# 272-token tiles padded to a multiple of 256 bytes, and the big buffers moved by 128 bytes against the weights

## The chip, the cores and the metric

The kernel runs on one core of one Trainium2 chip. The metric is the device time of one execution in microseconds; of several runs the median is given. A profile is one more execution, recorded by the hardware profiler; its span is the time from its first instruction to its last.

## The reference

One transformer block on 256 tokens of width 2048, with 16 meta tokens put in front (272 in all), in float32: a feed-forward block, a mixer with a pooling branch and a latent attention branch, and a second feed-forward block. Cut to what matters:

```python
h = concat([meta, x])                                   # 272 x 2048
h = h + 0.5 * rmsnorm(swiglu(rmsnorm(h), w_gu, w_down)) # 2 x 5632 columns, then 5632 rows
z = rmsnorm(h) @ w_in                                   # pool, c_q, c_kv, k_rope, two gates
y_pool = multiscale_pool(u_pool) @ w_pool_o
y_mla = attention(c_q @ w_q_b, c_kv @ w_kv_b, rope) @ w_mla_o
h = h + rmsnorm((sigmoid(g_pool) * y_pool + sigmoid(g_mla) * y_mla) @ w_out)
h = h + 0.5 * rmsnorm(swiglu(rmsnorm(h), w_gu2, w_down2))
return h[16:]
```

From the second half of the mixer on only the last 256 tokens are carried.

## The kernel before

Activations lie transposed: features on the 128 partitions, tokens along the free dimension, one tile per 128 features. A float32 product is made from parts of 12 bits: weight and input are each split into a high and a low part (`hi` and `lo`), and three products are added: high by high, high by low, low by high. With 272 tokens (`L`) these are three matmuls of 272 columns (`mm3`, lines 213 to 215). With 256 tokens (`R`) they are two (`mm_wide`): line 219 takes both parts of the input side by side, 512 columns, and line 221 the high part with the low part of the weight, 256 columns.

The weights are one stream of 128 x 128 tiles in the order of their use (class `Weights`). The DMA queue of SP loads chunks of `CH` = 8 tiles (512 KB) into one of `RAW` = 5 buffers (line 79). A part is `PT` = 4 tiles; for each part ACT makes the high half (line 92) and DVE the low half (line 93) in one of `HL` = 6 buffers. All this is issued by `take`, which is called once per tile just ahead of its matmuls:

```python
self.load((p + HL - 1) * PT // CH + RAW)
self.divide(p + min(HL - 1, p // 2 + 2))
```

So the splits of the weights stand in the queues of ACT and DVE between the work that empties PSUM. Each engine keeps the order in which its instructions are issued. `Later` delays work by a number of steps of the weights' stream.

Inputs of products are kept by class `Two`: eight tiles in a big buffer, each with its high part and then its low part. The big buffers come from one pool (`slot`, `SLOT` = 16 x 272 floats each, nine of them); one of them holds the residual stream `h` for the whole run. `big`, `raw`, `parts` and `tmp` (temporaries of 272 floats) lie one after another in the on-chip memory, the small ones ahead of them.

`products` runs over output tiles: where a block begins, `wave` = 6 of them side by side (their PSUM tiles are named `w`), with the input tiles coming up to date one by one (`Stream`), and then one by one (`m`), each over all input tiles. Names in the profile: `x` is a block's input, `a` the input of w_down, `o` the heads' output, `y` the gated sum, `po` the pooling branch's output product, `CB` the latent vectors of the attention. At the end of a block `post` and `advance` make the norm and the next input; `load_table` loads ACT's table of functions.

Of the kernel before, what the change touches and what calls it, by code (L numbers as in the profile page):

```python
# [27 lines left out]
CH, PT = 8, 4  # L28
RAW, HL = 5, 6
WARM = (3, 7)  # L30
# [6 lines left out]
C_COS, C_SIN, C_MASK, C_KPE, C_FREE = 0, 272, 544, 960, 1232  # L37
SLOT = KD * L


class Nothing:
    """Stands in for the builder's objects while the order of the weights is collected."""

# [16 lines left out]
class Weights:  # L60
    """The weights as one stream of [128, 128] tiles in the order of their use; each chunk of CH
    tiles is loaded ahead, and split, PT tiles at a time, into two parts of 12 bits, which together
    are the float32."""

# [32 lines left out]
    def take(self, *tiles):  # L97
        """The next tiles of the stream, side by side."""
        n = len(tiles)
        room = PT - len(self.order) % PT  # L100
        if room < n:
            self.order += [None] * room
        at = len(self.order)
        self.order += tiles
        if self.plan is None:
            return Nothing(), Nothing()
        assert self.plan[at : at + n] == list(tiles)
        p, j = divmod(at, PT)
        self.load((p + HL - 1) * PT // CH + RAW)
        self.divide(p + min(HL - 1, p // 2 + 2))  # L110
        for _ in tiles:
            self.tick()
        hi, lo = self.split[p]
        s = slice(j * P, (j + n) * P)
        return hi[:, s], lo[:, s]


class Later:
    """Work that is issued some steps of the weights' stream later, so that an engine isn't held
    by what another one has yet to do."""  # L120

# [3 lines left out]
    def __call__(self, *steps):  # L125
        """steps: pairs of a delay after the one before, and what to run then."""
        at = self.now
        for delay, run in steps:
            at += delay
            self.due.append((at, run))  # L130
        self.due.sort(key=lambda d: d[0])
# [11 lines left out]
def build(nc, tc, ctx, hT, wsrc, gains_d, const_d, tables_d, out, order):  # L143
# [7 lines left out]
    parts = ctx.enter_context(tc.tile_pool(name="parts", bufs=HL))  # L151
    big = ctx.enter_context(tc.tile_pool(name="big", bufs=9))
    tmp = ctx.enter_context(tc.tile_pool(name="tmp", bufs=6))
    psum = ctx.enter_context(tc.tile_pool(name="psum", bufs=8, space=bass.MemoryType.PSUM))
# [4 lines left out]
    def slot(cols, dt, name):  # L159
        t = big.tile([P, SLOT], dt, tag="S", name=name)  # L160
        return t[:, :cols]
# [9 lines left out]

# [1 line left out]
    h = slot3(KD, L, F32, "h")  # L173
    gains = keep.tile([P, NG], F32, tag="gains", name="gains")
# [19 lines left out]
    class Two:  # L194
        """n tiles of T tokens in two parts of 12 bits, side by side."""

        def __init__(self, n, T, name, src=None):
            self.T, self.at = T, 16 * T
            self.s = [src or slot(self.at, F32R, f"{name}{i}") for i in range(-(-n // 8))]
            self.s = [a[:, : self.at].rearrange("p (a b c) -> p a b c", a=8, b=2) for a in self.s]  # L200

# [15 lines left out]
    def mm_wide(b, w, x, k, first, last):  # L217
        """The same with the product of the low part of x in columns of its own, from R on."""
        mm(b.rearrange("p (b c) -> p b c", b=2), w[0], x.both(k, R), start=first, stop=last,  # L219
           skip_group_check=True)  # L220
        mm(b[:, :R], w[1], x.hi(k, R), start=False, stop=last, skip_group_check=True)  # L221

    def join(b, s):
        """s: the sum of both halves of b, in two steps."""
        act(s, b[:, R:], AF.Copy)
        return GAP, lambda: dve.tensor_tensor(s, b[:, :R], s, op=ALU.add)

    def warm(n, x=ident):
        """Keeps the tensor engine's clock up while it has to wait."""
        b = bank("warm")  # L230
        for _ in range(n):
            mm(b[:, :P], x[:, :P], x[:, :P], start=True, stop=True)

# [1 line left out]
    def rms_sums(sources, T, n, half=False):  # L235
        """1 / sqrt(mean + eps), or half of it, of the tokens whose squares' sums over the
        partitions of `sources` add up to n * mean; the tokens are on partitions."""
        b = bank("rms")
        tt = (0, P, L - P)[: 3 if T == L else 2]
        m, c0 = len(tt), 400  # L240
        for i, s in enumerate(sources):
            for j, t0 in enumerate(tt):
                mm(b[:, c0 + j : c0 + j + 1], s[:, t0 : t0 + P], ones[:, :1],
                   start=i == 0 and j == 0, stop=i == len(sources) - 1, skip_group_check=True)
        sd = tmp.tile([P, 4], F32, tag="sd", name="sd", bufs=2)
        f = 4 if half else 1
        act(sd[:, :m], b[:, c0 : c0 + m], AF.Sqrt, scale=f / n, bias=eps[:, f // 4 : f // 4 + 1])
        dve.reciprocal(sd[:, :m], sd[:, :m])
        return b, sd

    def rms_spread(b, sd, T):
        """The same for all partitions, in the bank's first T columns."""
        for j, (t0, c) in enumerate(((0, 0), (P, 0), (L - P, P - NMETA))[: 3 if T == L else 2]):
            mm(b[:, t0 + c : t0 + P], sd[:, j : j + 1].to_broadcast([P, P]), ident[:, c:],
               start=True, stop=True)
# [8 lines left out]
    def squares(src, T, j, last=False):  # L264
        """Adds the squares of src to acc; the last ones stay apart, for `rms` to add."""
        if j == 0:
# [11 lines left out]

# [1 line left out]
    class Stream:  # L280
        """The residual stream's parts for the next products; `update` brings a tile of it up to
        date. Issued in stages that lead the products by a tile."""

# [18 lines left out]
        def scale(self):  # L302
            """The pre-norm's scales; products of the unscaled input are scaled by them."""
            b, sd = rms_sums([acc] + self.last, self.T, DM)
# [6 lines left out]
    def products(names, n_k, x, T, wave, evac, stream=None, hooks={}, narrow=()):  # L311
        """Tiles of x @ w, transposed: the first `wave` of them side by side, then one by one."""
        wide = [T == R and i not in narrow for i in range(len(names))]
# [32 lines left out]

# [1 line left out]
    def post(names, n_k, x, T, g_post, half, wave, wait):  # L348
# [26 lines left out]

# [1 line left out]
    def ffn(x, w_gu, w_down, g_post, wait):  # L377
# [27 lines left out]

    # ================= first feed-forward =================
    warm(10, zero)
# [8 lines left out]

    # ================= mixer =================
    x = advance(t, b, L, G_MPRE)
# [15 lines left out]
    def rotate(o, src, T):  # L434
        """Rotary embedding of rows [x1, x2, x1, x2] of 32 each; o may not be src."""
        c = slice(L - T, L)
# [33 lines left out]
    def windows(j):  # L470
        """Difference of the windows' means and the input, in parts."""
        w = WINDOWS[j // 2]
# [19 lines left out]

    # columns of w_in in tiles: c_kv, k_rope twice, c_q, u_pool
    names = [("w_in", ("kv", j)) for j in range(4)] + [("w_in", ("kr", 0))]
# [57 lines left out]

# [1 line left out]
    o2 = Two(HEADS, R, "o")  # L554
# [40 lines left out]
    def proj_v(g):  # L595
        """Rows of v of four heads: tokens 0.., tokens 128.., and those from 256 on, by the high
        part of the input in rows 64.. and by the low part in rows 80.. ."""
        bs = [bank(f"v{i}") for i in range(3)]
# [47 lines left out]
    def turn(i):  # L646
        """Transposes the probabilities: keys 128.. and keys 0.. of the two times 128 queries. Of
        the first 128 queries' keys from 128 on only 16 exist, the rows below are zero; the second
        ones' keys from 256 on go to rows 64.. and again to rows 80.. of the last columns."""
        b = bank("pt")  # L650
# [49 lines left out]

# [1 line left out]
    y = Two(KD, R, "y")  # L702
# [17 lines left out]

    # ================= second feed-forward =================
    t, b = ffn(advance(t, b, R, G_F2PRE), "ffn2_w_gu", "ffn2_w_down", G_F2POST, (0, 0))
# [15 lines left out]
def columns(name, m):  # L738
    """Columns of a weight that make its tile m."""
    a = np.arange(P)  # L740
# [71 lines left out]
```

## Time and profile before

| | |
|---|---|
| time, median of 3 runs | 2244.32 us (2243.51 to 2244.43) |
| span of the profiled execution | 2257.5 us, granted PE clock 0.998 |
| PE busy | 2234.3 us (99%), 15040 matmuls |
| weight loads busy | 2062.4 us (91%) |
| DVE / ACT / POOL busy | 1362.2 / 1142.5 / 205.4 us |
| DMA | 393.46 MB, mean 174 GB/s, 53.7% of 16 engines' time for the weights' queue |

The profiled execution is 13.2 us (0.6%) longer than the median run. PE's rows are matmuls, PEld's the loads of their weights, which overlap them. A matmul's duration reaches from its start to its modelled end and overlaps the next one's, so the pace is read from one start to the next. In a tile's rows the columns are: line, engine, operation, out<-in, count, duration in ns (least, median, greatest), first and last start in us, shapes.

### The profile page before, as it was taken

To read this page: it belongs to the slowest core of one execution; us is meant where nothing else is said; L and a number is where in the kernel's file an instruction comes from. 1 tells how busy PE (TensorE), PEld (TensorE's weight loads), DVE (VectorE), ACT (ScalarE), POOL (GpSimd) and SP (SyncE) were. 2 spreads that over 40 slices of the span, in tenths; PEclk is the share of its full clock that TensorE was granted. 3 is DMA by queue.
4 is the path that set the end of the run, shared out by engine and by line. 5 is a ranking of instruction groups with operands and counts; after the bars stand their busy time and mean duration, and the time that the engine had idled before them with its cause. 6 is when DMAs were issued, how large, how long until landed. Compare 5 with 4: busy or idle time off the path is not lost.

```text
span 2257.5 us, 39449 instructions
## 1 busy us (share of the span) xinstructions
PE 2234.3 (99%) x15040; PEld 2062.4 (91%) x15040; DVE 1362.2 (60%) x2456; ACT 1142.5 (51%) x2273; POOL 205.4 (9%) x229
## 2 busy tenths in 40 slices
PE   9999999999999999999999999999999999999997
PEld 9999999999999999988888888888888888888886
DVE  6555555555444477766666677577666666654554
ACT  6444444444444454555544555665555555554543
POOL 2000000000000053200121111150000000000001
PEclk9999999999999999999999999999999999999999
DMA  6555555555555545566533356545655555655553
GB/s 242 178 175 174 179 172 178 177 170 177 177 169 180 175 150 168 178 190 188 173 113 122 114 169 195 186 151 186 185 188 184 188 186 186 187 191 187 187 182 117
DMA packets 109311, 393.46 MB, mean 174 GB/s; under 512 B 12288, under 2 KB 13696, under 8 KB 109120
## 3 DMA queue, kind: packets, MB, share of 16 engines
q1 hardware_dynamic: 108576, 389.19, 53.7%
q8 instruction: 118, 1.93, 0.4%
q0 software_dynamic: 400, 1.61, 0.2%
q14 instruction: 73, 0.60, 0.1%
q10 hardware_dynamic: 144, 0.13, 0.0%
HBM read 388.78 MB, written 2.10 MB: 173 GB/s over the span
## 4 chain that ended last, share of the span: by engine, by line
PE 97%; DVE 2%; issue 1%; DMA 0%; ACT 0%; SPq 0%; ACTq 0%; DVEq 0%
PE m L219 29%; PE m L221 15%; PE m L213 13%; PE m L215 12%; PE m L214 12%; PE w L219 2%; PE w L214 1%; PE w L221 1%; PE w L215 1%; PE s L622 1%; PE w L213 1%; PE po L213 1%; PE po L215 1%; PE po L214 1%; PE s L621 1%
## 5 line engine op out<-in xcount | busy, mean ns | idle before, releaser
L93 DVE TENSOR_TENSOR lo<-raw,hi 128x512 fp32r<-128x512 f32 x1472 | 1042.9, 722 | 691.7 <-ACT hi L92 686.7
L92 ACT ACTIVATE hi<-raw 128x512 fp32r<-128x512 f32 x1472 | 882.5, 625 | 393.6 <-PE m L214 283.1
L219 PE MATMUL m<-x,hi 128*128 128x512 f32 x1824 | 643.3, 398 | 0.0
L221 PE MATMUL m<-x,lo 128*128 128x256 f32 x1824 | 513.0, 281 | 0.0
L213 PE MATMUL m<-x,hi 128*128 128x272 f32 (+1 forms) x1488 | 429.6, 289 | 0.0
L215 PE MATMUL m<-x,lo 128*128 128x272 f32 (+1 forms) x1488 | 429.2, 288 | 0.0
L214 PE MATMUL m<-x,hi 128*128 128x272 f32 (+1 forms) x1488 | 428.4, 288 | 0.0
L219 PEld LDWEIGHTS m<-x,hi 128*128 128x128 f32 x1824 | 342.9, 188 | 83.2
L221 PEld LDWEIGHTS m<-x,lo 128*128 128x128 f32 x1824 | 345.0, 189 | 0.0
L214 PEld LDWEIGHTS m<-x,hi 128*128 128x128 f32 x1488 | 282.9, 190 | 0.0
L213 PEld LDWEIGHTS m<-x,hi 128*128 128x128 f32 x1488 | 279.8, 188 | 0.0
L215 PEld LDWEIGHTS m<-x,lo 128*128 128x128 f32 x1488 | 279.7, 188 | 0.0
L219 PE MATMUL m<-a,hi 128*128 128x512 f32 x660 | 233.2, 399 | 0.0
L273 POOL TENSOR_TENSOR acc<-acc,sq 128x272 f32<-128x272 f32 (+1 forms) x88 | 83.4, 948 | 1532.8 <-ACT sq L270 1532.5
L215 PE MATMUL m<-a,lo 128*128 128x272 f32 (+1 forms) x748 | 215.7, 288 | 0.0
L213 PE MATMUL m<-a,hi 128*128 128x272 f32 (+1 forms) x748 | 215.7, 288 | 0.0
L214 PE MATMUL m<-a,hi 128*128 128x272 f32 (+1 forms) x748 | 215.3, 288 | 0.0
L221 PE MATMUL m<-a,lo 128*128 128x256 f32 x660 | 185.4, 281 | 0.0
L219 PEld LDWEIGHTS m<-a,hi 128*128 128x128 f32 x660 | 124.1, 188 | 31.1
L214 PEld LDWEIGHTS m<-a,hi 128*128 128x128 f32 x748 | 142.4, 190 | 0.0
L213 PEld LDWEIGHTS m<-a,hi 128*128 128x128 f32 x748 | 140.8, 188 | 0.0
L215 PEld LDWEIGHTS m<-a,lo 128*128 128x128 f32 x748 | 140.8, 188 | 0.0
(206 smaller groups left out, 2577.4 us busy)
## 6 DMA issues: line engine op xcount, KB each, us to landing
raw<-w SPq DMA_DIRECT2D x735, 512.0 KB, 3.5
h<-hT POOLq DMA_DIRECT2D x4, 272.0 KB, 5.7
out<-t SPq DMA_DIRECT2D x8, 128.0 KB, 1.9
out<-t SPq DMA_DIRECT2D x4, 256.0 KB, 2.1
h<-hT SPq DMA_DIRECT2D x1, 544.0 KB, 9.1
raw<-w SPq DMA_DIRECT2D x2, 256.0 KB, 3.5
MA<-tables POOLq DMA_DIRECT2D x1, 480.0 KB, 3.7
h<-hT SPq DMA_DIRECT2D x2, 136.0 KB, 2.9
```

Of the source, the lines that this page charges most:

```text
L92: nc.scalar.activation(hi, t, AF.Copy)
L93: nc.vector.tensor_tensor(lo, t, hi.bitcast(F32), op=ALU.subtract)
L213: mm(o, wh, xh, start=first, stop=False)
L214: mm(o, wh, xl, start=False, stop=False)
L215: mm(o, wl, xh, start=False, stop=last)
L219: mm(b.rearrange("p (b c) -> p b c", b=2), w[0], x.both(k, R), start=first, stop=last, skip_group_check=True)
L221: mm(b[:, :R], w[1], x.hi(k, R), start=False, stop=last, skip_group_check=True)
L273: pool_e.tensor_tensor(acc[:, :T], acc[:, :T], s[:, :T], op=ALU.add)
L621: mm(b[:, c : c + n], q[:, t0 : t0 + P], k[:, :n], start=True, stop=False)
L622: mm(b[:, c : c + n], qp[hp : hp + 64, t0 : t0 + P], kpe[hp : hp + 64, :n], start=False, stop=True)
```

## The change

- `Two` gives each tile of 272 tokens `SIDE` = 32 floats of room behind its two parts, so that the step from tile to tile is 2304 bytes instead of 2176. Tiles of 256 tokens keep a step of 2048 bytes.
- A big buffer is `ROOM` = 18432 bytes instead of 17408. `h` gets a buffer of its own in a new pool ahead of the big ones, with 32 floats more than it needs; the pool `big` keeps eight buffers. By these sizes every big buffer now begins 128 bytes after a multiple of 256 bytes counted from the weights' parts; before it was 0.
- To make room, `RAW` goes from 5 to 4, `HL` from 6 to 5, and the temporaries from 6 to 5. Other sizes and the order of the matmuls are the same.
- Comments are gone and lines are numbered anew: lines 79, 92, 93 are 81, 94, 95 after; 213 to 215 are 219 to 221, and 219 and 221 are 225 and 227.

```diff
-RAW, HL = 5, 6
+RAW, HL = 4, 5
...
 SLOT = KD * L
+SIDE = 32
+ROOM = 8 * (2 * L + SIDE)
...
-    big = ctx.enter_context(tc.tile_pool(name="big", bufs=9))
-    tmp = ctx.enter_context(tc.tile_pool(name="tmp", bufs=6))
+    own = ctx.enter_context(tc.tile_pool(name="own", bufs=1))
+    big = ctx.enter_context(tc.tile_pool(name="big", bufs=8))
+    tmp = ctx.enter_context(tc.tile_pool(name="tmp", bufs=5))
...
-        t = big.tile([P, SLOT], dt, tag="S", name=name)
+        t = big.tile([P, ROOM], dt, tag="S", name=name)
...
-    h = slot3(KD, L, F32, "h")
+    h = own.tile([P, SLOT + SIDE], F32, tag="h", name="h")[:, :SLOT].rearrange("p (a b) -> p a b", a=KD)
...
         def __init__(self, n, T, name, src=None):
-            self.T, self.at = T, 16 * T
+            self.T, self.step = T, 2 * T + (SIDE if T == L else 0)
+            self.at = 8 * self.step
             self.s = [src or slot(self.at, F32R, f"{name}{i}") for i in range(-(-n // 8))]
-            self.s = [a[:, : self.at].rearrange("p (a b c) -> p a b c", a=8, b=2) for a in self.s]
+            self.s = [a[:, : self.at].rearrange("p (a c) -> p a c", a=8)[:, :, : 2 * T]
+                      .rearrange("p a (b c) -> p a b c", b=2) for a in self.s]
```

With `HL` smaller, each split stands one part earlier in the list of its engine's other work. ACT's instructions at the switch from w_mla_o to w_out (1397 us in the profile; `hi883` is the high half of part 883, `raw441` its chunk), before:

```order
L92 ACTIVATE hi882_16273<-raw441_16139 128x512
L711 ACTIVATE y1_15326<-zm_11200 128x256
L92 ACTIVATE hi883_16288<-raw441_16139 128x512
L225 ACTIVATE sum_16301<-m_16243 128x256
L711 ACTIVATE y1_15326<-zm_11200 128x256
L277 ACT_TABLE_LOAD
L277 ACTIVATE small_102<-eps_97 128x1
L92 ACTIVATE hi884_16316<-raw442_16166 128x512
L92 ACTIVATE hi885_16330<-raw442_16166 128x512
```

and after:

```order
L94 ACTIVATE hi881_16270<-raw440_16148 128x512
L717 ACTIVATE y1_15321<-zm_11195 128x256
L94 ACTIVATE hi882_16283<-raw441_16179 128x512
L231 ACTIVATE sum_16296<-m_16238 128x256
L717 ACTIVATE y1_15321<-zm_11195 128x256
L283 ACT_TABLE_LOAD
L283 ACTIVATE small_103<-eps_98 128x1
L94 ACTIVATE hi883_16313<-raw441_16179 128x512
L94 ACTIVATE hi884_16325<-raw442_16208 128x512
```

Before, part 883 is split ahead of the last sums and of the table load, after, behind them. The same on ACT at the second feed-forward's switch to w_down (1995 us), before:

```order
L394 ACTIVATE gu_22557<-gu_22557 128x256
L92 ACTIVATE hi1298_22589<-raw649_22456 128x512
L92 ACTIVATE hi1299_22603<-raw649_22456 128x512
L225 ACTIVATE gu_22615<-m_22559 128x256
L398 ACTIVATE a5_17309<-gu_22615 128x256
L277 ACT_TABLE_LOAD
L277 ACTIVATE small_102<-eps_97 128x1
L92 ACTIVATE hi1300_22625<-raw650_22483 128x512
```

and after:

```order
L400 ACTIVATE gu_22552<-gu_22552 128x256
L94 ACTIVATE hi1297_22586<-raw648_22466 128x512
L94 ACTIVATE hi1298_22598<-raw649_22495 128x512
L231 ACTIVATE gu_22610<-m_22554 128x256
L404 ACTIVATE a5_17304<-gu_22610 128x256
L283 ACT_TABLE_LOAD
L283 ACTIVATE small_103<-eps_98 128x1
L94 ACTIVATE hi1299_22622<-raw649_22495 128x512
```

Here part 1299 moves behind the table load. DVE's list moves in the same way. PE's list of matmuls, and SP's list of DMAs, are the same as before but for the buffers' numbers.

## The prediction

> **What bounds the kernel now.** I read the head of the page first, then the chain that ended last, then who made TensorE (PE) wait.
>
> ```profile
> span 2257.5 us, 39449 instructions
> ...
> PE 2234.3 (99%) x15040; PEld 2062.4 (91%) x15040; DVE 1362.2 (60%) x2456; ACT 1142.5 (51%) x2273; POOL 205.4 (9%) x229
> ...
> PEclk9999999999999999999999999999999999999999
> ...
> PE 97%; DVE 2%; issue 1%; DMA 0%; ACT 0%; SPq 0%; ACTq 0%; DVEq 0%
> ...
> L219 PE MATMUL m<-x,hi 128*128 128x512 f32 x1824 | 643.3, 398 | 0.0
> L221 PE MATMUL m<-x,lo 128*128 128x256 f32 x1824 | 513.0, 281 | 0.0
> ```
>
> PE is busy 99% of the span at a full granted clock, 97% of the chain is PE, and its big groups have no idle time before them. So what counts is the distance from one matmul's start to the next one's (durations overlap). Who PE waited for:
>
> ```profile
> PE w L219 <- DVE x L298: 3.6, 7, 0.7
> PE w L214 <- DVE x L298: 2.8, 6, 0.5
> PE warm L232 <- DVE zero L178: 1.2, 1, 1.2
> ```
>
> Under 8 us in all, at the start and where a block's output is added to the residual stream. The time is the pace of back-to-back matmuls. It stands in the rows of a tile, each with its count and the first and last start; in order: tile x at 60 to 580 us, tile a, tile x at 1050 to 1100 us, tile o, tile y, tile x at 1530 to 1990 us:
>
> ```profile
> L213 PE MATMUL m<-x,hi x1276: 284/288/293, 60.0 to 540.3; 128*128 128x272 f32 x183
> ...
> L219 PE MATMUL m<-a,hi x660: 394/398/404, 1992.7 to 2225.6; 128*128 128x512 f32 x165
> ...
> L219 PE MATMUL m<-x,hi x144: 392/394/397, 1049.7 to 1099.7; 128*128 128x512 f32 x144
> ...
> L219 PE MATMUL m<-o,hi x224: 390/391/392, 1316.6 to 1394.0; 128*128 128x512 f32 x112
> ...
> L219 PE MATMUL m<-y,hi x144: 394/398/404, 1428.1 to 1478.6; 128*128 128x512 f32 x144
> ...
> L219 PE MATMUL m<-x,hi x1303: 394/398/404, 1529.9 to 1989.9; 128*128 128x512 f32 x187
> ```
>
> Last start minus first, over the count less one: a **triple** of 272-token matmuls (lines 213, 214, 215) takes 480.3/1275 = 376.7 ns. A **pair** (512 columns at 219, 256 at 221) takes 460.0/1302 = 353.3 ns in the second feed-forward's x, 232.9/659 = 353.4 in a, 50.5/143 = 353.1 in y, but 77.4/223 = 347.1 in o and 50.0/143 = 350 in the gates. All are the same instructions; the pace differs by 2%.
>
> **Where the operands lie.** By the sizes in the code, every weight tile starts at the same place modulo 256 bytes (steps of 512, buffers of 4096 and 2048), and the big buffers (17408 = 68 x 256) too. So before, a 256-token operand lies 0 bytes from its weights modulo 256. A 272-token one steps by 2176 = 8.5 x 256: even tiles have their high part at 0 and their low part at 64, odd ones at 128 and 192. After, 272-token tiles are all at 128 and 192, 256-token ones at 128 (both parts); the gates, which read the last 256 of 272 tokens, go from 64 or 192 to 192 throughout.
>
> Does it matter? Two triples in a row of the first feed-forward, from the timeline (start, duration in us):
>
> ```profile
> 399.78 0.29 PE L213 MATMUL m<-x,hi 128*128 128x272 f32 x1
> ...
> 400.16 0.28 PE L213 MATMUL m<-x,hi 128*128 128x272 f32 x1
> ```
>
> Line 213's durations alternate between the ends of its 284 to 293 ns: along the order of the tiles the short ones (and triples of 372 ns) are the odd tiles, the long ones (381 ns) the even. But the mean need not move if all become odd: in the six side-by-side tiles at the start of the block, one input tile is used six times running. Starts of the first matmul of x tile 12, of tile 13 (odd), of the third triple of 13, and of tile 14:
>
> ```profile
> 35.41 0.29 PE L213 MATMUL w<-x,hi 128*128 128x272 f32 x1
> ...
> 37.67 0.29 PE L213 MATMUL w<-x,hi 128*128 128x272 f32 x1
> ...
> 38.42 0.29 PE L213 MATMUL w<-x,hi 128*128 128x272 f32 x1
> ...
> 39.94 0.29 PE L213 MATMUL w<-x,hi 128*128 128x272 f32 x1
> ```
>
> Even after even: 2.26/6 = 376.7 ns a triple. Odd after odd: 2.27/6 = 378.3, and its last four 1.52/4 = 380. So the gain of the odd tiles seems to be the other side of the even ones' loss.
>
> **The change part by part.**
> 1. *Pitch of 272-token tiles.* The triples that come one after another, from the groups by shape:
>
> ```profile
> L213 PE MATMUL m<-x,hi 128*128 128x272 f32 x1440 | 416.0, 289 | 0.0
> ...
> L213 PE MATMUL m<-a,hi 128*128 128x272 f32 x704 | 203.2, 289 | 0.0
> ```
>
> 2144 in all. Bounds from rows: all like the odd ones between even ones, 372 (-4.7 ns, -10.1 us), and all like the end of tile 13, 380 (+3.3, +7.1 us). I take 378.3, the odd-after-odd mean, since that is the layout after: 2144 x 1.6 = **+3.4 us**.
> 2. *256-token operands from 0 to 128.* Long pace: 1824 less the gates' 512 on x, 660 on a, 144 on y, and 2 x 96 side by side on x and y = 2308. No row shows a pair at 128. Bounds: the best pace of any pair, 347.1 (-6.2 ns, -14.3 us), and as far above 353.3 as that lies below, +14.3 us. I take 350, the nearest pairs that are not at 0 (the gates): 2308 x -3.3 = **-7.6 us**; and o's 256 pairs (with 32 side by side) from 347.1 to 350 too, **+0.7 us**. Gates, attention and narrow products change offset within what they span now: 0, within a microsecond or two.
> 3. *HL from 6 to 5.* Every split of a weight part (ACT's line 92, VectorE's (DVE) 93) is issued one part later. A part is four pairs, 1.41 us. Mostly this only shortens a lead: paired part by part along the stream, low parts are ready a median of 5.0 us ahead of their first use. Three places have under 1.41 us, each behind an activation table load. The clearest (ACT, PE, DVE rows, in order of time):
>
> ```profile
> 1397.08 1.28 ACT L277 ACT_TABLE_LOAD   x1
> ...
> 1398.46 0.39 PE L219 MATMUL w<-y,hi 128*128 128x512 f32 x1
> ...
> 1398.48 2.18 ACT L92 ACTIVATE hi<-raw 128x512 fp32r<-128x512 f32 x4
> ...
> 1398.69 0.28 PE L221 MATMUL w<-y,lo 128*128 128x256 f32 x1
> ...
> 1399.13 1.90 DVE L93 TENSOR_TENSOR lo<-raw,hi 128x512 fp32r<-128x512 f32 x3 [1.61 <-ACT hi L92]
> ...
> 1399.85 0.40 PE L219 MATMUL w<-y,hi 128*128 128x512 f32 x1
> ```
>
> Now the first split behind the load makes part 884, used from 1399.85 on. After, it makes 883, used from 1398.46, whose low part (ready at 1399.83) PE wants at 1398.69: 1.1 us of waiting. The same at the second feed-forward's switch to w_down:
>
> ```profile
> 1996.56 3.96 ACT L92 ACTIVATE hi<-raw 128x512 fp32r<-128x512 f32 x7
> ...
> 1997.20 0.28 PE L221 MATMUL m<-a,lo 128*128 128x256 f32 x1
> 1997.21 3.10 DVE L93 TENSOR_TENSOR lo<-raw,hi 128x512 fp32r<-128x512 f32 x5 [1.61 <-ACT hi L92]
> ```
>
> Its first low part (ready at 1997.90) belongs to one part earlier after, which PE wants at 1997.20: 0.7 us. At the sigmoid table (930 us) it is 0.7 again. Behind each, ACT makes parts faster than PE uses them (2.18/4 = 0.55 us each), so the wait comes once: **+2.5 us** (bounds 0, if ACT's work ahead ends earlier, and 3 x 1.41 = 4.2).
> 4. *RAW from 5 to 4.* A chunk lands in a median of 3.5 us and holds two parts, 2.8 us of PE; a buffer comes round after four chunks, 11.3 us. 7.8 us are left, so 0. DMA at half its time covers it:
>
> ```profile
> raw<-w SPq DMA_DIRECT2D x735, 512.0 KB, 3.5
> ```
>
> 5. *Five temporaries for six*: a gate lives some 28 steps of the weights' stream and a tile takes 16, so three are in use at once; 0. *h in a buffer of its own*: eight big ones are left, as before; 0. The pad is neither read nor written.
>
> Sum: +3.4 - 7.6 + 0.7 + 2.5 = -1.0 us, 2256.5 for the profiled execution. The median of the runs, 2244.32, lies 13.2 below the profiled span; I carry that over: **2243.3 us**. A change under 0.2%, 4.5 us, can hardly be told from none.
>
> **A rule against the trace.** The Trainium skill, "SBUF — State Buffer", section "Who interferes with whom", gives PE two independent read ports, one for the moving operand and one for weight loads, and says "PE and ACT never wait on anyone". By it no offset matters and parts 1 and 2 are 0; the rows of 372 and 381 ns speak against it within PE. Its page "TensorE: Matmul & The Clock Gate", section "Back-to-back issue gap", gives N/2.4 + 2.5 ns; estimated from that a pair would take 325 ns and a triple 347, so some 7% of PE's time would be there to win, were the offset all of it.
>
> **Rivals.**
> - *A: 128 is simply the good offset.* For it: the odd tiles' 372 ns. All triples at 372 and all long pairs at 347.1: -10.1 - 14.3 + 2.5 = -21.9, 2222 us; with one of the two 2232 to 2237. Against it: tile 13, and that o runs at 347.1 with offset 0, so one offset has two paces.
> - *B: the pace locks on the slow side.* With every tile at one offset the 272-token triples stay at the 380 ns of tile 13's end instead of alternating: +7.1, with +2.5 of waits and the pairs unmoved: +9.6, 2254 us. It decides the sign as long as the pairs win under 2.2 ns each (5.1 us). For it: the four triples at 380, and the two paces at one offset, which say that a stretch can stay where it started. Against it: tile 12's 376.7.
> - *C: offsets do nothing*, the difference is only phase: waits alone, +2.5, 2246.8 us. For it: equal means of alternating and of even-only triples. The port rule above says the same.
>
> **Chances.** The forecast 0.42; its own range, 2238 to 2250, lets 0.09 of it fall to faster and 0.04 to slower. A 0.26, faster. C 0.08, within 0.2%. B 0.24, slower. So faster 0.35, within 0.2% 0.37, slower 0.28. The range goes down to 2227 (A with most of both gains) and up to 2256 (B and a worse wait), and leaves about 0.1 on each side.
>
> **What would show it.** Right: tile rows of 394/398/404 become narrower and pairs take near 350; triples 377 to 380 with no two kinds; PE idles before w L219 or L221 for ACT hi or DVE lo at 930, 1398 and 1997 us. Wrong: pairs at 347 or under, or triples at 372 (A); pairs above 353 (B); long waits for raw, which would be part 4.

## The result, and the profile after

The change makes the kernel slower: 2259.94 us (2256.58 to 2263.35, four runs) against 2244.38 (2243.51 to 2246.22), a ratio of 1.0068, 95% interval 1.0054 to 1.0083. The forecast of 2243.3 and its range up to 2256 missed it. The four runs are of two kinds, near 2256.6 and near 2263.2; the profile is of the 2256.58 run. The profiled execution alone says something else: its span is 2254.8 us, 2.7 *below* the 2257.5 of the profile before.

The page's first lines and the two large groups of pairs (lines 225 and 227 are 219 and 221 of before):

```profile
span 2254.8 us, 39608 instructions
...
PE 2230.4 (99%) x15040; PEld 2064.8 (92%) x15040; DVE 1363.2 (60%) x2456; ACT 1141.6 (51%) x2273; POOL 205.2 (9%) x229
...
L225 PE MATMUL m<-x,hi 128*128 128x512 f32 x1824 | 639.1, 393 | 0.1
L227 PE MATMUL m<-x,lo 128*128 128x256 f32 x1824 | 514.1, 282 | 0.2 <-DVE lo L95 0.2
```

PE is as busy as before, so again the pace decides. The tile rows after: triples at 60 to 530 us, gates at 1050 to 1100, o, y, x of the second feed-forward at 1545 to 1975, and a at 2010 to 2205:

```profile
L219 PE MATMUL m<-x,hi x1248: 288/290/293, 60.1 to 529.8; 128*128 128x272 f32 x179
...
L225 PE MATMUL m<-x,hi x145: 392/392/392, 1049.8 to 1099.7; 128*128 128x512 f32 x145
...
L225 PE MATMUL m<-o,hi x224: 387/396/398, 1316.0 to 1394.3; 128*128 128x512 f32 x112
...
L225 PE MATMUL m<-y,hi x144: 387/396/398, 1429.6 to 1479.8; 128*128 128x512 f32 x144
...
L225 PE MATMUL m<-x,hi x1226: 387/396/398, 1544.9 to 1975.0; 128*128 128x512 f32 x176
...
L225 PE MATMUL m<-a,hi x556: 387/396/398, 2010.0 to 2204.8; 128*128 128x512 f32 x186
```

Triples: 469.7/1247 = 376.7 ns, as before. Pairs: 78.3/223 = 351.1 in o, 50.2/143 = 351.0 in y, 430.1/1225 = 351.1 in x, 194.8/555 = 351.0 in a: one pace in place of two. The gates run at 49.9/144 = 346.5 instead of 350. The waits behind the table loads came; PE's timeline at the switch to w_out:

```profile
1398.70 0.28 PE L227 MATMUL w<-y,lo 128*128 128x256 f32 x1
1399.47 0.49 PE L225 MATMUL w<-y,hi 128*128 128x512 f32 x1 [0.48 <-ACT hi L94]
1400.19 0.39 PE L227 MATMUL w<-y,lo 128*128 128x256 f32 x1 [0.23 <-DVE lo L95]
1400.41 0.40 PE L225 MATMUL w<-y,hi 128*128 128x512 f32 x1
```

The next start comes 0.77 us on instead of 0.12, the one after it 0.72 on instead of 0.23: 1.14 us lost, where 1.1 was forecast. The two other places lose 0.8 each.

So against the profile before, pairs and waits behave nearly as forecast; the triples, forecast to lose, stay as they were, and the gates, set to 0, gain. What did not hold is that this profile stands for the runs of before. Run times and spans of the changed kernel lie 1.8 us apart (2256.58 and 2254.8), so a profile of 2257.5 belongs to an execution of 2259.3 us, not to one of 2244. The first question was what an execution of 2244 looks like.

### The profile page after: what moved, and what is told of

The parts are those of the page before. It is cut to its first block, busy times and chain, and to the rows that moved or that the text cites. A ratio compares the mean times of both kernels' runs of the same rounds, so it can differ in the third digit from the quotient of the medians.

```text
span 2254.8 us, 39608 instructions
## 1 busy us (share of the span) xinstructions
PE 2230.4 (99%) x15040; PEld 2064.8 (92%) x15040; DVE 1363.2 (60%) x2456; ACT 1141.6 (51%) x2273; POOL 205.2 (9%) x229
## 4 chain that ended last, share of the span: by engine, by line
PE 96%; DVE 2%; issue 1%; ACT 0%; POOL 0%; DMA 0%; SPq 0%; ACTq 0%; POOLq 0%
PE m L225 29%; PE m L227 15%; PE m L219 13%; PE m L221 12%; PE m L220 12%; PE w L225 1%; PE w L220 1%; PE w L221 1%; PE w L219 1%; PE s L628 1%; PE w L227 1%; PE po L220 1%; PE po L219 1%; PE po L221 1%; PE s L627 1%
```

## The experiments

All times are medians; each kernel was compared with runs of the kernel before on the same chip.

**The kernel before, again.** No edit.

> The kernel before, unchanged, to see which pace its executions run at. Theory P (locked pace): at offset 0 the pairs of 256-token products have two paces, 346.7 ns and 353.3 ns; runs of 2244 us run all 2308 + 256 pairs at 346.7, and the first profiled execution (span 2257.5 us) was one that fell to 353.3 from 1400 us on: 2308 x 6.67 = 15.4 us. So a profiled execution of some 2242 us shows pairs of 347 throughout, one of 2257 shows 353. Theory S (the profiler costs 13 us): timed runs 2244 us while the profiled span stays at 2257 us with pairs at 353.

Measured: ten runs, seven at 2244.1 to 2245.9 us and three at 2258.4 to 2259.0; of 31 runs of the kernel before beside it, 24 near 2246 and seven near 2258.7. The profile is of a run of 2245.51 us, with a span of 2243.7. Its tile rows, in order o, y, x, a:

```profile
L219 PE MATMUL m<-o,hi x224: 391/391/391, 1316.0 to 1393.3; 128*128 128x512 f32 x112
...
L219 PE MATMUL m<-y,hi x144: 395/398/403, 1427.4 to 1478.0; 128*128 128x512 f32 x144
...
L219 PE MATMUL m<-x,hi x1241: 392/395/395, 1544.8 to 1974.7; 128*128 128x512 f32 x178
...
L219 PE MATMUL m<-a,hi x564: 392/394/395, 2009.7 to 2204.9; 128*128 128x512 f32 x188
```

x runs at 429.9/1240 = 346.7 ns and a at 195.2/563 = 346.7, where the first profile had 353.3 and 353.4. y is on the long pace in both (50.5/143 = 353.1 in the first profile, 50.6/143 = 353.8 here; the starts in a row are rounded to 0.1 us, which is 0.7 ns over 143 pairs). 1312 + 660 = 1972 pairs by 6.67 ns are 13.1 us, of the 13.8 between the two spans (2257.5 and 2243.7): this is what the prediction carried over, as 13.2, as if it were the profiler's. The theory that profiling costs 13 us falls. Theory P had y at 346.7 too, which is wrong: in this trace the pairs go over from 346.7 to 353.3 ns between o and y, at 1399.2 to 1399.5 us, with the first pair of the part that was split first behind the table load (part 884 of the prediction). PE shows no idle time there; whether a delay too short to be listed sets it off, no run shows.

**Offsets alone.** An unused tile ahead of the big buffers; the temporaries, which lie behind them, move along, and all else is as before:

```diff
+    gap = ctx.enter_context(tc.tile_pool(name="gap", bufs=1))
+    gap.tile([P, 16], F32, tag="gap", name="gap")     # 16, 32 or 48 floats: 64, 128, 192 bytes
     big = ctx.enter_context(tc.tile_pool(name="big", bufs=9))
```

> The kernel before with an unused tile of 64 bytes ahead of the big buffers: all of them 64 bytes from the weights modulo 256; all buffers, pads and the order as before. Theory P: the pairs get a pace of this offset's own, between 346.7 and 353.3 ns (the gates ran at 349 and 351): 2244 to 2257 us; triples stay at 376.7. Theory W (the smaller number of buffers costs the time, the offset nothing): 2244 us.

> The same with 128 bytes, the offset of the change, but without its pad and with all buffers as before. Theory P: pairs at 351.1 ns as in the profile after, 2564 x 4.4 = 11.3 us more than runs at 346.7: 2255 us, no waits at the table loads. Theory W: 2244 us. If the pad matters (theory T), triples differ from 376.7 by some ns, 2144 x 1 ns = 2.1 us each.

> The same with 192 bytes. Theory P: another pace between 346.7 and 353.3 ns: 2244 to 2257 us. Theory W: 2244 us.

Measured: 2265.55, 2254.77 and 2253.26 us against 2246.02; ratios 1.0068 (1.0049 to 1.0088), 1.0021 (1.0001 to 1.0040), 1.0014 (0.9994 to 1.0033). The intervals are wide because the runs of before beside them were of both kinds; all thirty runs are slower than each of its 24 usual ones (at most 2246.57). The ten runs of each of the three lie within 1.3 us, none of a second kind. Tile rows of the triples and of x's pairs at 64, 128 and 192 bytes:

```profile
L215 PE MATMUL m<-x,hi x1237: 287/288/293, 60.1 to 529.8; 128*128 128x272 f32 x177
...
L221 PE MATMUL m<-x,hi x1218: 392/397/398, 1544.7 to 1974.7; 128*128 128x512 f32 x174
```

```profile
L215 PE MATMUL m<-x,hi x1248: 285/288/292, 59.9 to 529.6; 128*128 128x272 f32 x179
...
L221 PE MATMUL m<-x,hi x1226: 387/396/398, 1544.9 to 1975.0; 128*128 128x512 f32 x176
```

```profile
L215 PE MATMUL m<-x,hi x1256: 283/288/291, 60.0 to 529.9; 128*128 128x272 f32 x180
...
L221 PE MATMUL m<-x,hi x1218: 397/397/398, 1544.8 to 1974.8; 128*128 128x512 f32 x174
```

| offset, bytes | triples, ns | pairs on x, ns | time, us |
|---|---|---|---|
| 0 | 376.7 | 346.7 or 353.3 | 2246 or 2259 |
| 64 | 380.0 | 353.3 | 2265.6 |
| 128 | 376.7 | 351.1 | 2254.8 |
| 192 | 374.4 | 353.3 | 2253.3 |

(Each pace is last start less first over count less one.) The offset alone, with all buffers kept and no pad, costs the pairs 4.4 ns each over the usual pace at 0, and is most of what the change loses. W, which put the loss on the buffers alone, falls. The triples gain nothing at 128, as at 0. At 64 theory P missed: it had the triples unmoved and the time at 2257 at most.

For the pairs the first column is the offset of every operand. For the triples it is that of the first tile of a buffer only, since the tiles alternate by 128 bytes. At 64 and at 192 the tiles so lie at the same two offsets, in swapped order, and yet take 380.0 and 374.4 ns: the offset from the weights modulo 256 bytes does not by itself fix the pace of the triples. What does is open.

**Smaller buffers alone, and pad with smaller buffers at offset 0.**

```diff
-RAW, HL = 5, 6
+RAW, HL = 4, 5                       # buf: with own pool for h, big 8, tmp 5; no pad, no SIDE in h
```

```diff
-    h = own.tile([P, SLOT + SIDE], F32, tag="h", name="h")[:, :SLOT].rearrange("p (a b) -> p a b", a=KD)
+    h = own.tile([P, SLOT], F32, tag="h", name="h")[:, :SLOT].rearrange("p (a b) -> p a b", a=KD)   # pad0: the changed kernel with the big buffers at 0 again
```

> The kernel before with the smaller buffers of the change alone: RAW 4, HL 5, five temporaries, h in a buffer of its own; no pad, all offsets 0. Theory P: triples 376.7, the three waits behind the table loads cost 2.5 us, and these waits may flip the pairs between 346.7 and 353.3 ns: 2247 us where they stay at 346.7, 2262 where not. Theory W: the buffers carry the loss: 2260 us with the pairs at 346.7.

> The changed kernel with h 128 bytes smaller, so that all big buffers lie at offset 0 again: pad and smaller buffers alone. 272-token tiles are then all at 0 (high part) and 64 (low part). Theory P: pairs have the two paces of offset 0 (346.7 or 353.3), triples 376.7 to 378: with waits of 2.5 us 2246 to 2250 us, or 15 us more where the pairs lock at 353.3. If the pad cost the time (theory T): 2260 us with pairs at 346.7 and triples above 380.

Measured: 2256.23 and 2255.56 us against 2244.57, ratios 1.0054 (1.0039 to 1.0069) and 1.0046 (1.0031 to 1.0061): slower without any offset. x and then a, of buf and of pad0:

```profile
L220 PE MATMUL m<-x,hi x1218: 395/398/403, 1544.8 to 1974.8; 128*128 128x512 f32 x174
...
L220 PE MATMUL m<-a,hi x564: 392/394/395, 2009.7 to 2204.9; 128*128 128x512 f32 x188
```

```profile
L225 PE MATMUL m<-x,hi x1242: 392/394/395, 1544.7 to 1974.9; 128*128 128x512 f32 x178
...
L225 PE MATMUL m<-a,hi x553: 395/398/403, 2009.9 to 2204.9; 128*128 128x512 f32 x185
```

In buf x has the long pace and a the short one, in pad0 the other way round, so both times lie between the two that theory P gave for each. In both profiles of the kernel before a follows x at x's pace; here a wait lies between them, at the table load of the switch to w_down. So a wait costs its own length and also lets the stretch behind it lock anew. Why x of buf ran long isn't shown: no wait that the change brings lies just ahead of it. The numbers fit: 1312 x 6.67 = 8.8 us and 2.7 us of waits, less 1.0 for y, which ran short, make 10.5 of the 10.8 us between buf's span and again's (2254.5 and 2243.7). The triples of pad0, whose tiles all begin at 0, take 470.1/1246 = 377.3 ns:

```profile
L219 PE MATMUL m<-x,hi x1247: 285/288/292, 59.8 to 529.9; 128*128 128x272 f32 x179
```

**HL alone, and a shifted start without any such wait.**

```diff
-RAW, HL = 5, 6
+RAW, HL = 5, 5                       # hl5
```

```diff
-    t, b = post([("w_out", m) for m in range(KD)], KD, y, R, G_MPOST, False, 6, WARM)
+    t, b = post([("w_out", m) for m in range(KD)], KD, y, R, G_MPOST, False, 6, (3, 8))   # warm8; 6 and 9 alike
```

> The kernel before with HL 5 alone: RAW 5, six temporaries, all offsets 0. Theory H (history: a wait for a weight part restarts the stretch of products behind it, and at offset 0 a stretch locks at 346.7 or 353.3 ns): three waits, 2.5 us in all; behind each a stretch with either pace: 2246 us if x of the second feed-forward (1312 pairs) and its a (660 pairs) both stay at 346.7, 8.8 us more if x locks at 353.3, 4.4 us more if a does. Theory W (RAW or the temporaries carry the loss of the smaller buffers): 2246 us with paces as in the runs of before.

> The kernel before with one filling matmul less (6 instead of 7) ahead of the second feed-forward; nothing else: no offset and no buffer changes. Theory H: the phase in which the 1312 pairs on x begin is another, so they may lock at 353.3 ns instead of 346.7: 2245 or 2254 us; if a locks anew too, up to 2258 us. Theory F (the pace is fixed by offsets and buffers): 2244 us, x at 346.7.

> The same with one filling matmul more (8). Theory H: 2245 or 2254 us by the pace of x. Theory F: 2244 us.

> The same with two more (9). Theory H: 2245 or 2254 us by the pace of x. Theory F: 2244 us.

Measured for hl5: 2251.61 us (2247.23 to 2252.21) against 2244.41, ratio 1.0028 (1.0017 to 1.0039). Two runs lie at 2247.2 and 2247.8, six at 2251.4 to 2252.2. The profile is of the 2247.23 run: x at 346.7, a at 346.7 (row below), y short as well, and three waits. At the three places the starts of this trace lie 2.8 us further apart than again's, and that is the price of HL's waits alone. The other six lie 4.4 us higher, the 660 pairs of a at 353.3 (4.4 us); that is inferred, none of the six was profiled.

```profile
L219 PE MATMUL m<-a,hi x564: 391/391/391, 2009.7 to 2204.8; 128*128 128x512 f32 x188
```

The three warm kernels ran at 2244.39, 2244.57 and 2245.38 us, ratios 1.0000, 0.9995 and 0.9995, each interval around 1: shifting the start of x by some matmuls does not choose its pace. One of nine runs of warm8 took 2258.65 us and is the profiled one, with x and a both at the long pace; two of 29 runs of before beside it did so too. So the choice differs from execution to execution, and H's form of it, by the phase of the start, isn't shown.

**The changed kernel, four more executions.** Its runs had two kinds, 2256.6 and 2263.2 us.

> The changed kernel, unchanged, to see its second kind of execution: its runs lay at 2256.6 or 2263.2 us, and the profile was of the first kind (pairs 351.1 ns, triples 376.7). Theory P: the second kind has one part of the products locked at another pace, either the 2144 triples at 380 instead of 376.7 (7.1 us) or the 2564 pairs at 353.3 instead of 351.1 (5.7 us). Theory W: the 6.6 us are waits for weight parts.

> The changed kernel once more, for its second kind of execution (2263.2 us beside 2256.6). Theory H: in a profile near 2261.5 us one kind of product runs at another pace: the 2144 triples at 380 instead of 376.7 ns (7.1 us), or the pairs at 353.3 instead of 351.1 (2.2 ns each, 5.2 us for x, a and o); waits stay at three, 2.6 us. Theory W: the paces are those of the first kind and the 6.6 us are waits for weight parts.

> As after_c: theory H another pace of the triples (7.1 us) or of the pairs (5.2 us) if the time is near 2263, theory W waits; near 2256.6 us the paces of the first kind.

> As after_c: theory H another pace of the triples (7.1 us) or of the pairs (5.2 us) if the time is near 2263, theory W waits; near 2256.6 us the paces of the first kind.

Measured: after_again 2256.69 us (three near it, one at 2263.23; ratio 1.0058, 1.0043 to 1.0073), after_c 2256.55, after_e 2256.23, and after_d 2262.52. Triples of after_d, and its pairs on x:

```profile
L219 PE MATMUL m<-x,hi x1238: 289/289/290, 59.9 to 529.9; 128*128 128x272 f32 x177
...
L225 PE MATMUL m<-x,hi x1225: 386/396/398, 1544.9 to 1974.7; 128*128 128x512 f32 x175
```

after_c, after_d and after_e are single runs; the one run of the kernel before beside them took 2258.20 us, its longer kind. 470.0/1237 = 380.0 ns a triple in after_d, 376.7 in the others; pairs and waits are the same. From the first triple on x to the first feed-forward's last on a this costs 6.7 us; after_d's start is 0.7 shorter, which makes the 6.0 between the two spans (2260.8 and 2254.8). The second kind has the pace that rival B named: all triples at 380, as at the end of tile 13 in the profile before. Without the pad no execution showed it at offset 128 (ten runs of off128 within 1.1 us); with all tiles at one offset four of eleven runs have its time. But one offset for all tiles isn't needed for 380: off64 ran at it with alternating tiles.

**Each product at its best offset.** RAW 4 pays for the room; HL 6 and six temporaries stay.

```diff
-RAW, HL = 5, 6
+RAW, HL = 4, 6
...
+EDGE = 48
+ROOM = SLOT + 64
...
-        t = big.tile([P, SLOT], dt, tag="S", name=name)
+        t = big.tile([P, ROOM], dt, tag="S", name=name)
...
+            e = EDGE if T == L else 0
-            self.s = [src or slot(self.at, F32R, f"{name}{i}") for i in range(-(-n // 8))]
+            self.s = [src or slot(e + self.at, F32R, f"{name}{i}")[:, e:] for i in range(-(-n // 8))]
```

> Each kind of product at the offset at which it ran best: 272-token tiles begin 192 bytes from the weights (triples 374.4 ns at that offset), 256-token ones at 0 (346.7 where they lock there). RAW 4 makes room, HL 6 and six temporaries stay, so that no wait comes behind the table loads. Theory P: paces add up: 2144 x 2.2 = 4.8 us under the kernel before, 2240 us, or 2254 us where the pairs lock at 353.3. Theory S (paces come from the stretch's history, not from its own offset): triples 376.7, 2245 us.

Measured: 2240.80 us (2240.20 to 2241.13, ten runs) against 2244.57, ratio 0.9982, 0.9972 to 0.9992: faster than both kernels. Triples, x, a:

```profile
L217 PE MATMUL m<-x,hi x1256: 282/287/289, 60.0 to 529.9; 128*128 128x272 f32 x180
...
L222 PE MATMUL m<-x,hi x1241: 392/392/395, 1544.8 to 1974.7; 128*128 128x512 f32 x178
L222 PE MATMUL m<-a,hi x564: 392/394/395, 2009.7 to 2204.9; 128*128 128x512 f32 x188
```

374.4 ns (469.9/1255) and twice 346.7. The triples' gain of 2.2 ns by 2144 is 4.8 us, 3.8 were measured. RAW 4 and the lead of HL 6 cost nothing that shows.

## Why the prediction was wrong, and where it held

- **The step that failed** is "The median of the runs, 2244.32, lies 13.2 below the profiled span; I carry that over". The profiled execution had 353.3 ns on x and a, the usual runs 346.7 (13.1 us on 1972 pairs). A run and its own span differ by 1.8 us, the other way round. Against the usual run the pairs do not win 3.3 ns, they lose 4.4: 9.7 us on x, a and o, less 0.3 on y. The hint stood in the profile: o at 347.1 and x at 353.3 with the same operands' offset. The prediction used it for a bound and for rival B ("a stretch can stay where it started") and did not ask at which pace the runs went.
- **Sum against the profile before: near, in part by luck.** -1.0 forecast, -2.7 measured. Pairs on x, a, y: 351.1 instead of 350 (2116 x -2.2 = -4.7 us, against -7.6). o up by 4.0 on 224 pairs, +0.9, against +0.7. The pairs' miss of 2.9 and the triples' of 3.4 cancel.
- **Triples: size off.** +3.4 forecast, 0 in the usual execution; in the rarer ones +6.7, near rival B's 7.1. The 1.6 ns a triple came from 2.26 against 2.27 us over six triples, one step of the last digit shown; the trace's own starts are 2.266 and 2.267 us apart, so that reading carried nothing.
- **Waits: right.** +2.5 forecast, 2.7 measured, at the three places named and for the part named. What was missed is their second effect, shown at offset 0: the stretch behind locks anew.
- **Gates: missed.** Set to 0, they gained 1.3 us: 3.2 ns on the last 256 of their 512 pairs, 1.8 to 2.5 on the others.
- **RAW, temporaries, h: 0 as forecast**, shown for RAW by mix; hl5's waits and stretches of pairs account for buf without the rest.
- **The sum against the usual run**: pairs on x, a and o +9.7, y -0.3, waits +2.7, gates -1.3: 10.8 of the 11.1 us between the spans 2243.7 and 2254.8. The median of 2259.94 lies higher because two of its four runs were of the kind near 2263.2, in which after_d had the triples at 380; these two were not profiled themselves. The runs near 2256.6 miss the range too.
- **Rivals.** A (128 is the good offset) is wrong: the odd tiles' 372 ns were the other side of the even ones' 381. C (offsets do nothing), and with it the rule on PE's ports in the Trainium skill's page "SBUF — State Buffer", section "Who interferes with whom", as far as it was taken to exclude any effect of the offset: off64 takes 2265.6 us by its offset alone, so here the measurement decides. The formula of the Trainium skill's page "TensorE: Matmul & The Clock Gate", section "Back-to-back issue gap", from which the prediction estimates 325 and 347 ns, is given there for an isolated matmul, not for a stream with weight loads. No stretch read here came below 346.7 ns a pair and 374.4 a triple, so the 7% to be won stays unshown. Off128's loss with all buffers kept was not among the rivals; B had the sign, by another mechanism.

## What to carry to other kernels

Before a profile's sum is carried to the runs' median, ask whether the profiled execution is of the same kind as the runs: a span some tenths of a per cent off is a finding, not a constant. Read the pace of back-to-back instructions stage by stage (first start, last start, count), and where like stages differ, expect the pace to differ between executions too and take another profile. An address change is judged by the mean over the whole repeating pattern, since a slow tile next to a fast one can be one rhythm.

## What the runs showed of the hardware

A stretch of back-to-back matmuls with weight loads keeps one pace for hundreds of microseconds (here x, 430 us, and a, 195 us). The pace depends on where the moving operands begin, in steps of 64 bytes. For pairs it is 346.7 or 353.3 ns at offset 0, 353.3 at 64, 351.1 at 128, 353.3 at 192. For triples it is 374.4 to 380.0 ns, and their offset alone doesn't fix it. All offsets here are counted from the weights modulo 256 bytes; no run moved the weights, so it isn't shown that the distance counts, and not the operand's own address.

At offset 0 a pair has two paces. No kept trace shows a change within x or a; behind a wait, or where a new block begins, the pace may be another one, and between o and y it changes without any idle time listed. On x of the second feed-forward it differs between executions of one program.

The paces can be written, to 0.1 ns, as whole multiples of 6.667 ns over one to six repeats: 346.67 = 52, 353.33 = 53, 380.0 = 57, twice 376.67 = 113, three times 351.11 = 158, five times 377.33 = 283, six times 374.44 = 337. This is arithmetic on the rows: the unit is the step from 346.7 to 353.3, and with so many repeats allowed a fit proves little. What has that period, and how it meets the two streams of reads, no run here shows.
